# A two-layer token mixer on one core: other byte distances between matrix operands, other places for some halves, and row statistics by other instructions

## Chip, core and metric

The kernel runs on one core of a Trainium2 chip. The metric is the device time of one execution in microseconds (us); the kernel before takes 889.34 us, the median of 3 runs. The engines of the core are named as in the profile: PE is TensorE's matrix multiply and PEld its weight load, DVE is VectorE, ACT is ScalarE, POOL is GpSimd and SP the engine that issues most loads.

## What is computed

The reference runs two layers on 512 tokens of width 1024 (`x`) and, in the first layer, on 256 context tokens (`ctx`). Layer 0 is a retention mixer with four heads, layer 1 a gated mixer. Cut to what matters:

```
h  = rmsnorm(x, g) * (1 + scale) + shift            # per layer, from the conditioning vector
# layer 0, per head: q, k (256 wide), v, z (512 wide) = h @ w_in
o  = (q k^T * decay) v ;  o = o / rms(o) ;  x += gate * ((o * silu(z)) @ w_out)
# layer 1: u, v, z (2048 wide each) = h @ w_in
v  = v - mean(v, axis=-1)                            # over all 2048 columns of a token
v  = v * rsqrt(mean(v * v, axis=-1) + 1e-6) * vnorm_g
mixed = w_s[group] @ v[chunk of 128 tokens] + b_s
x += gate * ((u * mixed * silu(z)) @ w_out)
out = rmsnorm(x, final_g)
```

All inputs, weights and the output are float32.

## The kernel before

**Products.** A large product is made of seven half-size products of sums and differences of quarters (B11, B21, T1, T2, B22, T3, T4; a name that begins with T takes a difference of two weight quarters). Every float32 operand is split into a high part, rounded to the format that PE reads (a copy by ACT), and a low part, the rest (a subtraction by DVE); `mm3` then issues three matmuls: low by high, high by low, high by high. A weight quarter is loaded into a raw tile (`w0` and so on), for a T name subtracted on DVE, and split into one of four `hl` tiles. `Stream.get` (`Q.get`) hands the tiles out in order and keeps two more in preparation.

**Two forms.** `Product` (`features`, for q/k and for u/z of layer 1) keeps the weights stationary and streams 256 columns of activations. `Pair` (`tokens`, for v and z of layer 0 and v of layer 1, called V01, Z01, V23, Z23 and V1 below) keeps the activations (`oA..`, `oS..`, `hc`, and `rows` for the context) stationary and streams 512 columns of the split weight. The probabilities by v (`ph`, `pl` by `v`) and the last projection (`ya`, `yb` by `hl`) also stream 512 columns. `Pair.ended` copies banks by ACT into `snap` tiles (KEPT), adds to them by DVE (MADE) and calls `done`; for the quarter "21" the bank itself is handed over.

**Where tiles lie.** The loop over `(tag, size, bufs)` at the head of the kernel reserves SBUF in that order, sizes in float32 elements per partition. Counted from the first `hl` tile, modulo 256 bytes: an `hl` room has 8448 bytes, 33 times 256, so all four start at 0, and the split weight starts `FORMS` elements behind that: 32 bytes for kq, u and wo, 96 for v, z and v1, 128 for o. The eleven `t2` tiles (`snap`, `ph`, `pl`, `vt`, ...) are at 0; `cv` takes 64 bytes; so all `o..` tiles, `hc`, `g2`, `g3`, `s0`, `s2`, `s3` and `w4` are at 64, and behind `gate0` (32 bytes) `s1`, `rope`, the other `w` tiles and `dec` are at 96.

**Order.** PE follows the order of the text (`pe.kept = True`). From the end of the first stage on ACT and DVE do not (`act.kept = dve.kept = False`): a scheduler orders their instructions by the text as far as their operands and tiles are free, except behind `fence`. A tile that takes over the place of another one waits until the other one's last reader in the text is done.

**Places the change touches.** In V01 the sums of quarters come between the products (`sums`): `sum_s4` and `rows_s2` at T1, `sum_s3` at T2. The context rows lie in `w7` (S1), `s1` (S2), `s3` (S4) and `s0` (S3). The quarters of the activations lie in `s0` to `s3`: f11 in `s0`, f12 in `s1`, f21 in `s2`, f22 in `s3`; `sum_s3` subtracts f21 from f11 and is the last reader of f21. `load_qk(0)` and `load_v(0)` are generators that load and split (`halves`) q, k and v of head 0: they are stepped by `aside` during Z23 and, for what is left, at the first steps of `attend(0)`. `load_qk` has three steps of loads and five of halves, `load_v` four of loads and three of halves. In V1 `v1_done` puts two `bn_stats` of DVE per bank into a list (`measured`), which the loop over `TURNS1` works off; behind the loop come `bn_aggr`, a square root on ACT, a reciprocal and `nb`; `norm_vt(0)` scales the first v tiles, which the first pass over u multiplies behind its product B22.

Of the kernel before, what the change touches and what calls it, by code (L numbers as in the profile page):

```python
# [68 lines left out]
def hybrid_kernel(ctx, tc, xT_d, cT_d, cv_d, sv_d, rows_d, ada0_d, adag_d, w_d, rope_d, dec_d, ws_d, id_d, out_d):  # L69
# [13 lines left out]
    def st(shape, tag, dt=F32, bufs=1, name=None):  # L83
        return sb.tile(shape, dt, tag=tag, name=name or tag, bufs=bufs)

    T2 = 11
    HL = 4
    FORMS = {"kq": 8, "u": 8, "wo": 8, "v": 24, "z": 24, "v1": 24, "o": 32}


    for tag, size, bufs in (("hl", 2112, HL), ("t2", 512, T2), ("cv", 16, 1),
                            *((f"o{k}", 2048, 1) for k in ("A11", "A12", "A22", "S1", "S2", "S3", "S4")), ("hc", 4096, 1),
                            *((k, 1024, 1) for k in ("g2", "g3", "s0", "s2", "s3", "w4")), ("gate0", 8, 1),
                            *((k, 1024, 1) for k in ("s1", "rope", "w5", "w6", "w0", "w1", "w2", "w3", "w7", "g1", "g0")), ("dec", TW, 1)):
        st([P, size], tag, bufs=bufs, name="room")
# [43 lines left out]
    class Stream:  # L139
# [3 lines left out]
        def __init__(self):  # L143
            self.items, self.loads, self.raws, self.left, self.tiles = [], [], {}, {}, {}
            self.free, self.stage, self.done, self.sent, self.at = [], 0, 0, 0, -1
            self.gate = self.limit = self.cap = None
# [65 lines left out]
            return self.tiles.pop(self.at)  # L212

    Q = Stream()
    W = [f"w{i}" for i in range(7)]
    Q.free += W + ["g0"]

    def narrow_parts(a, b, kh):
# [160 lines left out]
    class Pair:  # L379

        def __init__(self, done, rows=None):
            self.done, self.rows, self.s, self.banks = done, rows, {}, {}

        def run(self, name, c, w):
            role = ROLE.get(name, "x")
# [15 lines left out]
        def ended(self, name, t, bank):  # L403
            if name in KEPT:
                k = self.s[KEPT[name], t] = t2("snap")
                act.copy(k, bank)
            elif name in MADE:
                key, to = MADE[name]
                k = self.s.pop((key, t))
                dve.tensor_tensor(k, bank, k, ALU.add)  # L410
                self.done(to, t, k)
            else:
                self.done("21", t, bank)
# [15 lines left out]
            load(xq[t, g], xT_d[:, 4 * g:4 * g + 4, t * HS:t * HS + HS])  # L429

    ada_w = {}
    ADA_AT = ("oS1", "oS2", "oS4", "oA22", "oS1", "oS2", "oS4", ("w7", "g1"))

    def ada0_load(kb):
        at = ADA_AT[kb]
# [357 lines left out]
    def rows_s1():  # L793
        dve.tensor_tensor(c22, c21, c22, ALU.add)
        dve.tensor_tensor(shc, sh0[:, 0:4, 1], sh0[:, 4:8, 1], ALU.add)
        rows_shifted("S1", "w7", shc)

    def rows_s2():
        dve.tensor_tensor(c22, c22, c11, ALU.subtract)
        rows_shifted("S2", "s1", sh0[:, 4:8, 1])  # L800

    def rows_s4():
        dve.tensor_tensor(c12, c12, c22, ALU.subtract)
# [194 lines left out]
    for q, name in TURNS:  # L998
        if q not in prods:
            prods[q] = project(q)  # L1000
            if q == Z23:
                Q.free.append("g0")
                qk0, v0 = load_qk(0), load_v(0)
        for c, unit in enumerate(units(q)):
            i = turn[q] = turn.get(q, -1) + 1
            if q[0] == "kq":
                prods[q].run(name, Q.get())
            else:
                prods[q].run(name, c, Q.get())
            if q == V01:  # L1010
                for made in sums.get((name, c), ()):
                    made()
                if c and name not in ("B11", "T1"):
                    popped()
                continue
            if i % 2:
                popped()
            if 1 not in pieces and (i % 2 if q == Z01 else q == V23 or i == 0):
                pieces.append(step())
            if q == V23 and i in (6, 8, 10, 12):  # L1020
                if i == 6:
                    dec0 = decay(0, ("g0", "s2"))
                aside(dec0)
            if q == Z23:
                if i in (0, 1, 2, 5, 7, 9):
                    aside(qk0)
                if i in (2, 4, 6, 11, 12):
                    aside(v0)
        if (q, name) == (V01, "T4"):
            Q.free.remove("g0")  # L1030
# [6 lines left out]
    def attend(h, qs, vs):  # L1037
# [83 lines left out]
        for i in range(len(steps) + LAG):  # L1121
            if i < len(steps):
                score(*steps[i])
            if i >= LAG:
                pv(*steps[i - LAG])
            if i == 2:
                aside(table())
            aside(qs)
            if i > 4 or h == 0 and i < 2:
                aside(vs)  # L1130
            if i == len(steps):
                flip()
            if (h, i) == (0, 2):
                for c in range(4):
                    load(acc[:, 2 * c:2 * c + 2, :], xT_d[:, 2 * c:2 * c + 2, :])
            if i < 5:
                aside(wo)
            if i in (3, 5, 6) or (h and i == 7):
                step()
# [149 lines left out]
    project_out(wos.pop(HEADS - 1), og, flip, (), then=half_sum, between=first_half, prepare=prepare)  # L1289


    bns = st([P, NT, 8, 6], "bns")
    measured = []

    def v1_done(p):
        def done(name, t, c):
            if name == "21":
                k = t2("snap")
                act.copy(k, c)
                c = k  # L1300
            n, nh = 2 * (int(name[0]) - 1) + t, int(name[1]) - 1
            measured.append(lambda: [dve.bn_stats(bns[:, n, 4 * p + 2 * j + nh, :], c[:, j * HS:j * HS + HS]) for j in range(2)])
            spill(vt_d[p][nh][:, :, n, :], c.rearrange("p (j n) -> p j n", j=2))
        return done

    rest1 = second_half()
    pairs = [Pair(v1_done(p)) for p in range(2)]
    for p, name in TURNS1:
        for c in range(2):
            pairs[p].run(name, c, Q.get())  # L1310
            while len(measured) > (4 if (p, name) in [(0, n) for n in PAIRED[:-1]] else 0):
                measured.pop(0)()
            if p == 0 and (c == 0 and name in ("B11", "B21", "T1", "T2", "B22") or (name, c) == ("B11", 1)):
                next(rest1)
        if (p, name) == (0, "B21"):
            residual()
# [3 lines left out]
    load(wsT, ws_d)  # L1320
    fg = st([P, D], "g0", name="fg")
    load(fg, rows_d[1:2, :].partition_broadcast(P))

    mv = st([P, NT, 2], "mv")
    for t in range(NT):
        dve.bn_aggr(mv[:, t, :], bns[:, t, :, :])
    rv = st([P, NT], "rv")
    act.activation(rv, mv[:, :, 1], AF.Sqrt, bias=eps, scale=1.0)
    dve.reciprocal(rv, rv)

    o1 = [st([P, D], f"s{t}", name="o1") for t in range(NT)]
    ya = st([P, 4, 2, SEQ], "hc", F32R, name="ya")
# [92 lines left out]
    def load_vt(i):  # L1425
        vts[i] = []
        for th in range(2):
            v = t2("vt", (P, 2, HS))
            load(v, vt_d[i // 4][i % 2][:, i // 2 % 2, 2 * th:2 * th + 2, :])
            vts[i].append(v)  # L1430

    nb = st([P, NT], "nb")
    dve.scalar_tensor_tensor(nb, mv[:, :, 0], -1.0, rv, ALU.mult, ALU.mult)

    def norm_vt(i):
        for n in range(NT):
# [26 lines left out]
        split((y[:, 0, :], y[:, 1, :]), a)  # L1463

    load_vt(0)
    norm_vt(0)
    for i in range(UZ):
        got, pms = {}, {}
        prod = Product(features, got.__setitem__)
        for name in SINGLE:  # L1470
            w = Q.get()
            settle()
            prod.run(name, w)
            if i < UZ - 1:
                if name == "T1":
                    load_vt(i + 1)
                if name == "T4":
                    norm_vt(i + 1)
# [122 lines left out]
```

## Time and profile before

| | |
|---|---|
| median of 3 runs | 889.34 us (889.31 to 889.42) |
| the profiled execution | 890.13 us, of it 888.4 us from the first to the last instruction |
| granted PE clock | 0.999 |
| PE / PEld / DVE / ACT busy | 98% / 88% / 81% / 52% of the span |
| DMA | 153.78 MB, 173 GB/s on average |

The profiled execution is 0.8 us longer than the median, 0.1%. All instructions carry line 55, the helper that records them, so groups are told apart by their tiles (written tile, then read ones) and shapes. The duration of a matmul is its own passage through the array; the next one starts before it ends, so the cost of one in a row of them is the distance between two starts: a block of n matmuls that is shown with its length lasts n - 1 such spacings and one duration.

### The profile page before, as it was taken

To read this page: it belongs to the slowest core of one execution; us is meant where nothing else is said; L and a number is where in the kernel's file an instruction comes from. 1 tells how busy PE (TensorE), PEld (TensorE's weight loads), DVE (VectorE), ACT (ScalarE), POOL (GpSimd) and SP (SyncE) were. 2 spreads that over 40 slices of the span, in tenths; PEclk is the share of its full clock that TensorE was granted. 3 is DMA by queue.
4 is the path that set the end of the run, shared out by engine and by line. 5 is a ranking of instruction groups with operands and counts; after the bars stand their busy time and mean duration, and the time that the engine had idled before them with its cause. 6 is when DMAs were issued, how large, how long until landed. Compare 5 with 4: busy or idle time off the path is not lost.

```text
span 888.4 us, 14615 instructions
## 1 busy us (share of the span) xinstructions
PE 873.1 (98%) x5670; PEld 778.8 (88%) x5670; DVE 722.8 (81%) x1016; ACT 463.1 (52%) x727; POOL 55.8 (6%) x92
## 2 busy tenths in 40 slices
PE   8999999999999999999999999999999999999997
PEld 7888898898889888999989898878999899899895
DVE  2689979988796977878687869999898578778986
ACT  5465444544524566536462559563765455255244
POOL 0001110110121020000000011102000000000000
PEclk9999999999999999999999999999999999999999
DMA  9931761972794586758175721546345045045202
GB/s 334 390 124 52 251 218 56 300 248 87 241 350 145 196 290 198 263 162 299 47 253 177 243 73 72 164 144 213 127 135 168 24 144 167 23 143 198 88 25 94
DMA packets 77092, 153.78 MB, mean 173 GB/s; under 512 B 8032, under 2 KB 35040, under 8 KB 77024
## 3 DMA queue, kind: packets, MB, share of 16 engines
q1 hardware_dynamic: 69888, 130.63, 44.9%
q0 software_dynamic: 6848, 22.03, 6.6%
q8 instruction: 44, 0.72, 0.4%
q10 hardware_dynamic: 288, 0.20, 0.1%
q14 instruction: 24, 0.20, 0.1%
HBM read 128.71 MB, written 24.12 MB: 172 GB/s over the span
## 4 chain that ended last, share of the span: by engine, by line
PE 88%; DVE 6%; ACT 3%; DMA 2%; issue 1%; SPq 0%; ACTq 0%; DVEq 0%
PE pst L55 88%; DVE hl L55 2%; DMA xq<-in_xT_dram 2%; DVE o L55 1%; DVE raw L55 1%; ACT hl L55 1%; DMA xs<-x 1%; DVE bns L55 1%; ACT f L55 0%; ACT oA L55 0%; ACT junk L55 0%; DVE ya L55 0%; DVE xq L55 0%; SPq L129 0%; ACT o L55 0%
## 5 line engine op out<-in xcount | busy, mean ns | idle before, releaser
L55 DVE TENSOR_TENSOR hl<-raw,hl 128x1024 fp32r<-128x1024 f32 x195 | 236.2, 1221 | 67.3 <-ACT hl L55 66.5
L55 ACT CAST hl<-raw 128x1024 fp32r<-128x1024 f32 x195 | 203.7, 1050 | 160.2 <-PE pst L55 63.5
L55 PE MATMUL pst<-hl,oS 128*128 128x512 f32 x576 | 137.9, 395 | 0.0
L55 PE MATMUL pst<-oS,hl 128*128 128x256 f32 x1104 | 134.7, 280 | 2.4 <-DVE hl L55 1.8
L55 PEld LDWEIGHTS pst<-oS,hl 128*128 128x128 f32 x1104 | 131.2, 188 | 3.6 <-DVE hl L55 2.2
L55 PEld LDWEIGHTS pst<-hl,oS 128*128 128x128 f32 x576 | 107.7, 187 | 27.0 <-DVE oS L55 0.4
L55 PE MATMUL pst<-oA,hl 128*128 128x256 f32 x936 | 118.2, 281 | 0.2
L55 PEld LDWEIGHTS pst<-oA,hl 128*128 128x128 f32 x936 | 112.8, 188 | 2.4 <-issue 0.8
L55 DVE TENSOR_TENSOR raw<-raw 128x1024 f32<-128x1024 f32 x92 | 111.3, 1219 | 0.8
L55 PE MATMUL pst<-hl,oA 128*128 128x512 f32 x408 | 98.6, 395 | 1.4 <-DVE hl L55 1.4
L55 PEld LDWEIGHTS pst<-hl,oA 128*128 128x128 f32 x408 | 76.0, 187 | 19.9 <-DVE hl L55 1.9
L55 PE MATMUL pst<-og,hl 128*128 128x256 f32 x768 | 92.8, 280 | 0.0
L55 PEld LDWEIGHTS pst<-og,hl 128*128 128x128 f32 x768 | 90.9, 188 | 0.8 <-issue 0.4
L55 ACT COPY snap<-pst 128x512 f32<-128x512 f32 x88 | 51.5, 587 | 70.1 <-PE pst L55 69.9
L55 PE MATMUL pst<-hl,ya 128*128 128x512 f32 (+1 forms) x300 | 69.4, 384 | 0.0
L55 PEld LDWEIGHTS pst<-hl,ya 128*128 128x128 f32 x300 | 54.7, 188 | 11.5
L55 PE MATMUL pst<-v,ph 128*128 128x512 f32 x192 | 59.7, 392 | 0.0
L55 DVE TENSOR_TENSOR snap<-pst,snap 128x512 f32<-128x512 f32 x75 | 51.2, 687 | 9.6 <-PE pst L55 9.0
L55 PEld LDWEIGHTS pst<-v,ph 128*128 128x128 f32 x192 | 36.1, 188 | 7.5
L55 ACT CAST ph<-pf 128x512 fp32r<-128x512 f32 x24 | 14.9, 622 | 51.0 <-DVE pf L55 48.3
L55 PE MATMUL pst<-v,pl 128*128 128x512 f32 x96 | 38.2, 398 | 0.0
L55 PEld LDWEIGHTS pst<-qk 128*128 128x128 f32 x288 | 35.8, 188 | 2.7 <-issue 1.6
(186 smaller groups left out, 990.6 us busy)
## 6 DMA issues: line engine op xcount, KB each, us to landing
raw<-in_w_dram SPq DMA_DIRECT2D x224, 256.0 KB, 4.3
bg<-in_adag_dram SPq DMA_DIRECT2D x32, 512.0 KB, 5.1
ada_w<-in_ada_dram SPq DMA_DIRECT2D x16, 512.0 KB, 8.9
raw<-in_w_dram SPq DMA_DIRECT2D x16, 512.0 KB, 3.9
bg<-in_dec_dram SPq DMA_DIRECT2D x12, 512.0 KB, 5.1
v<-snap POOLq DMA_DIRECT2D x16, 256.0 KB, 4.7
z<-snap POOLq DMA_DIRECT2D x16, 256.0 KB, 5.4
v<-v SPq DMA_DIRECT2D x8, 512.0 KB, 5.0
```

The source lines that it names most:

```text
L55: made = op(*args, **kw)
```

## The change

Five parts. (1) `FORMS` puts the split weights of v, z, v1 and o at element 16 (64 bytes), and `cv` is reserved ahead of `t2`, so `t2` tiles lie at 64 as well; the rows S1 and S2 move to `w4` and `s2`, both at 64. Every stationary tile that is used with 512 streamed columns then lies at the same place modulo 256 bytes as the streamed one ("row distance 0"). (2) `w7` and `w4` change roles in the list of raw tiles and in the first stage's loads, and the decay table of head 0 passes through `g0` and `s1`. (3) The remaining halves of q and k of head 0 (two steps) and one more of v are called at step 12 of Z23, and `attend(0)` steps `vs` at its first step only, not at two. (4) In V1 the sum of a block's 512 columns comes out of the addition that makes it (`scalar_tensor_tensor` with `accum_out`), or out of ACT's copy for "21"; ACT squares each block around the block's own mean with an accumulator (`AF.Square`, 16 of them) in place of 32 `bn_stats`. (5) Mean and variance are put together by `spread_v`, called behind T2 of the first pass over u together with `norm_vt(0)`; what is left in `measured` is worked off one per turn, and at that T2 all of it.

```diff
@@ -85,10 +85,10 @@
 
     T2 = 11
     HL = 4
-    FORMS = {"kq": 8, "u": 8, "wo": 8, "v": 24, "z": 24, "v1": 24, "o": 32}
-
-
-    for tag, size, bufs in (("hl", 2112, HL), ("t2", 512, T2), ("cv", 16, 1),
+    FORMS = {"kq": 8, "u": 8, "wo": 8, "v": 16, "z": 16, "v1": 16, "o": 16}
+
+
+    for tag, size, bufs in (("hl", 2112, HL), ("cv", 16, 1), ("t2", 512, T2),
                             *((f"o{k}", 2048, 1) for k in ("A11", "A12", "A22", "S1", "S2", "S3", "S4")), ("hc", 4096, 1),
                             *((k, 1024, 1) for k in ("g2", "g3", "s0", "s2", "s3", "w4")), ("gate0", 8, 1),
                             *((k, 1024, 1) for k in ("s1", "rope", "w5", "w6", "w0", "w1", "w2", "w3", "w7", "g1", "g0")), ("dec", TW, 1)):
@@ -212,7 +212,7 @@
             return self.tiles.pop(self.at)
 
     Q = Stream()
-    W = [f"w{i}" for i in range(7)]
+    W = ["w0", "w1", "w2", "w3", "w7", "w5", "w6"]
     Q.free += W + ["g0"]
 
     def narrow_parts(a, b, kh):
@@ -380,8 +380,8 @@
 
 
 
-        def __init__(self, done, rows=None):
-            self.done, self.rows, self.s, self.banks = done, rows, {}, {}
+        def __init__(self, done, rows=None, total=None):
+            self.done, self.rows, self.total, self.s, self.banks = done, rows, total, {}, {}
 
         def run(self, name, c, w):
             role = ROLE.get(name, "x")
@@ -407,7 +407,10 @@
             elif name in MADE:
                 key, to = MADE[name]
                 k = self.s.pop((key, t))
-                dve.tensor_tensor(k, bank, k, ALU.add)
+                if self.total:
+                    dve.scalar_tensor_tensor(k, bank, 0.0, k, ALU.add, ALU.add, accum_out=self.total(to, t))
+                else:
+                    dve.tensor_tensor(k, bank, k, ALU.add)
                 self.done(to, t, k)
             else:
                 self.done("21", t, bank)
@@ -429,7 +432,7 @@
             load(xq[t, g], xT_d[:, 4 * g:4 * g + 4, t * HS:t * HS + HS])
 
     ada_w = {}
-    ADA_AT = ("oS1", "oS2", "oS4", "oA22", "oS1", "oS2", "oS4", ("w7", "g1"))
+    ADA_AT = ("oS1", "oS2", "oS4", "oA22", "oS1", "oS2", "oS4", ("w4", "g1"))
 
     def ada0_load(kb):
         at = ADA_AT[kb]
@@ -793,11 +796,11 @@
     def rows_s1():
         dve.tensor_tensor(c22, c21, c22, ALU.add)
         dve.tensor_tensor(shc, sh0[:, 0:4, 1], sh0[:, 4:8, 1], ALU.add)
-        rows_shifted("S1", "w7", shc)
+        rows_shifted("S1", "w4", shc)
 
     def rows_s2():
         dve.tensor_tensor(c22, c22, c11, ALU.subtract)
-        rows_shifted("S2", "s1", sh0[:, 4:8, 1])
+        rows_shifted("S2", "s2", sh0[:, 4:8, 1])
 
     def rows_s4():
         dve.tensor_tensor(c12, c12, c22, ALU.subtract)
@@ -1019,12 +1022,12 @@
                 pieces.append(step())
             if q == V23 and i in (6, 8, 10, 12):
                 if i == 6:
-                    dec0 = decay(0, ("g0", "s2"))
+                    dec0 = decay(0, ("g0", "s1"))
                 aside(dec0)
             if q == Z23:
-                if i in (0, 1, 2, 5, 7, 9):
+                for _ in range({0: 1, 1: 1, 2: 1, 5: 1, 7: 1, 9: 1, 12: 2}.get(i, 0)):
                     aside(qk0)
-                if i in (2, 4, 6, 11, 12):
+                for _ in range({2: 1, 4: 1, 6: 1, 11: 1, 12: 2}.get(i, 0)):
                     aside(v0)
         if (q, name) == (V01, "T4"):
             Q.free.remove("g0")
@@ -1126,7 +1129,7 @@
             if i == 2:
                 aside(table())
             aside(qs)
-            if i > 4 or h == 0 and i < 2:
+            if i > 4 or h == 0 and i < 1:
                 aside(vs)
             if i == len(steps):
                 flip()
@@ -1289,26 +1292,37 @@
     project_out(wos.pop(HEADS - 1), og, flip, (), then=half_sum, between=first_half, prepare=prepare)
 
 
-    bns = st([P, NT, 8, 6], "bns")
+    vsum = st([P, NT, 4], "vsum")
+    vmid = st([P, NT, 4], "vmid")
+    vsq = st([P, NT, 4], "vsq")
     measured = []
+
+    def v1_total(p):
+        def total(name, t):
+            n, nh = 2 * (int(name[0]) - 1) + t, int(name[1]) - 1
+            return vsum[:, n, 2 * p + nh:2 * p + nh + 1]
+        return total
 
     def v1_done(p):
         def done(name, t, c):
+            n, b = 2 * (int(name[0]) - 1) + t, 2 * p + int(name[1]) - 1
             if name == "21":
                 k = t2("snap")
-                act.copy(k, c)
+                act.activation(k, c, AF.Copy, accum_out=vsum[:, n, b:b + 1])
                 c = k
-            n, nh = 2 * (int(name[0]) - 1) + t, int(name[1]) - 1
-            measured.append(lambda: [dve.bn_stats(bns[:, n, 4 * p + 2 * j + nh, :], c[:, j * HS:j * HS + HS]) for j in range(2)])
-            spill(vt_d[p][nh][:, :, n, :], c.rearrange("p (j n) -> p j n", j=2))
+            if t == 1:
+                dve.tensor_scalar(vmid[:, n - 1:n + 1, b], vsum[:, n - 1:n + 1, b], -1.0 / 512, None, ALU.mult)
+            measured.append(lambda: act.activation(t2("junk1"), c, AF.Square, bias=vmid[:, n, b:b + 1], scale=1.0,
+                                                   accum_out=vsq[:, n, b:b + 1]))
+            spill(vt_d[p][int(name[1]) - 1][:, :, n, :], c.rearrange("p (j n) -> p j n", j=2))
         return done
 
     rest1 = second_half()
-    pairs = [Pair(v1_done(p)) for p in range(2)]
+    pairs = [Pair(v1_done(p), total=v1_total(p)) for p in range(2)]
     for p, name in TURNS1:
         for c in range(2):
             pairs[p].run(name, c, Q.get())
-            while len(measured) > (4 if (p, name) in [(0, n) for n in PAIRED[:-1]] else 0):
+            if len(measured) > (4 if p == 0 else 2):
                 measured.pop(0)()
             if p == 0 and (c == 0 and name in ("B11", "B21", "T1", "T2", "B22") or (name, c) == ("B11", 1)):
                 next(rest1)
@@ -1320,13 +1334,6 @@
     load(wsT, ws_d)
     fg = st([P, D], "g0", name="fg")
     load(fg, rows_d[1:2, :].partition_broadcast(P))
-
-    mv = st([P, NT, 2], "mv")
-    for t in range(NT):
-        dve.bn_aggr(mv[:, t, :], bns[:, t, :, :])
-    rv = st([P, NT], "rv")
-    act.activation(rv, mv[:, :, 1], AF.Sqrt, bias=eps, scale=1.0)
-    dve.reciprocal(rv, rv)
 
     o1 = [st([P, D], f"s{t}", name="o1") for t in range(NT)]
     ya = st([P, 4, 2, SEQ], "hc", F32R, name="ya")
@@ -1429,8 +1436,21 @@
             load(v, vt_d[i // 4][i % 2][:, i // 2 % 2, 2 * th:2 * th + 2, :])
             vts[i].append(v)
 
+    rv = st([P, NT], "rv")
     nb = st([P, NT], "nb")
-    dve.scalar_tensor_tensor(nb, mv[:, :, 0], -1.0, rv, ALU.mult, ALU.mult)
+
+    def spread_v():
+        mean = st([P, NT], "mean")
+        var = st([P, NT], "var")
+        dve.tensor_reduce(mean, vsum, axis=AX.X, op=ALU.add)
+        dve.tensor_scalar(mean, mean, 1.0 / 2048, None, ALU.mult)
+        dve.tensor_tensor(vmid, vmid, mean.unsqueeze(2).to_broadcast([P, NT, 4]), ALU.add)
+        dve.tensor_tensor(vmid, vmid, vmid, ALU.mult)
+        dve.scalar_tensor_tensor(vsq, vmid, 512.0, vsq, ALU.mult, ALU.add)
+        dve.tensor_reduce(var, vsq, axis=AX.X, op=ALU.add)
+        act.activation(rv, var, AF.Sqrt, bias=eps, scale=1.0 / 2048)
+        dve.reciprocal(rv, rv)
+        dve.scalar_tensor_tensor(nb, mean, -1.0, rv, ALU.mult, ALU.mult)
 
     def norm_vt(i):
         for n in range(NT):
@@ -1463,7 +1483,6 @@
         split((y[:, 0, :], y[:, 1, :]), a)
 
     load_vt(0)
-    norm_vt(0)
     for i in range(UZ):
         got, pms = {}, {}
         prod = Product(features, got.__setitem__)
@@ -1471,6 +1490,13 @@
             w = Q.get()
             settle()
             prod.run(name, w)
+            if measured:
+                measured.pop(0)()
+            if i == 0 and name == "T2":
+                while measured:
+                    measured.pop(0)()
+                spread_v()
+                norm_vt(0)
             if i < UZ - 1:
                 if name == "T1":
                     load_vt(i + 1)
```

## Prediction

> **What bounds the kernel now.** I read the page first, then the waits of PE.
>
> ```profile
> PE 873.1 (98%) x5670; PEld 778.8 (88%) x5670; DVE 722.8 (81%) x1016; ACT 463.1 (52%) x727; POOL 55.8 (6%) x92
> ```
>
> ```profile
> PE pst L55 <- DVE hl L55: 3.2, 3, 1.4
> PE pst L55 <- issue: 1.4, 1, 1.4
> ```
>
> PE is busy for 98% of the span, and its waits add up to a few us, of which three of about 1.4 us are most. So time can come from two sources: the spacing of PE's matmuls, and these three waits. For the spacing I took the groups with shapes kept apart (each the number of its matmuls behind the x) and then blocks of the timeline.
>
> ```profile
> L55 PE MATMUL pst<-hl,oS 128*128 128x512 f32 x576 | 137.9, 395 | 0.0
> ...
> L55 PE MATMUL pst<-hl,oA 128*128 128x512 f32 x408 | 98.6, 395 | 1.4 <-DVE hl L55 1.4
> ...
> L55 PE MATMUL pst<-hl,ya 128*128 128x512 f32 x276 | 66.6, 394 | 0.0
> L55 PE MATMUL pst<-v,ph 128*128 128x512 f32 x192 | 59.7, 392 | 0.0
> L55 PE MATMUL pst<-v,pl 128*128 128x512 f32 x96 | 38.2, 398 | 0.0
> ```
>
> ```profile
> L55 PE MATMUL pst<-hl,rows 128*128 128x512 f32 x96 | 24.7, 392 | 0.0
> L55 PE MATMUL pst<-hl,yb 128*128 128x512 f32 x96 | 24.6, 391 | 0.0
> ```
>
> ```profile
> L55 PE MATMUL pst<-hl,hc 128*128 128x512 f32 x72 | 18.7, 395 | 0.0
> ```
>
> In the kernel before, `rows` S1 and S2 (in `w7`, `s1`, at 96) meet an `hl` at 96, distance 0, while `rows` S4 and S3 (`s3`, `s0`, at 64) meet it 32 bytes apart. The same holds within one pass, so it is an experiment that the old kernel makes by itself: below, the block at 92.02 is S2, that at 96.19 is S4.
>
> ```profile
> 92.02 1.53 PE L55 MATMUL pst<-hl,rows 128*128 128x512 f32 x6
> 93.39 2.96 PE L55 MATMUL pst<-hl,oS 128*128 128x512 f32 x12
> 96.19 1.56 PE L55 MATMUL pst<-hl,rows 128*128 128x512 f32 x6
> ```
>
> ```profile
> 537.44 2.90 PE L55 MATMUL pst<-hl_e,oA 128*128 128x512 f32 x12
> ```
>
> A block of n lasts n - 1 spacings and one duration of 0.39. S2: (1.53 - 0.393)/5 = 227.4 ns; S4: (1.56 - 0.393)/5 = 233.4 ns; the twelve at 93.39 (distance 32): (2.96 - 0.395)/11 = 233.2 ns. The `hl_e` tiles lie in `oA22` and `oS2`, at 64 like their `oA11`, so distance 0 again: (2.90 - 0.389)/11 = 228.3 ns. Last, the distance of 64 (`ya` with an `o` weight at 128, `v` at 64 with `ph`, `pl` at 0):
>
> ```profile
> 685.48 22.57 PE L55 MATMUL pst<-hl,ya 128*128 128x512 f32 x96
> ```
>
> ```profile
> 754.99 1.54 PE L55 MATMUL pst<-hl,ya 128*128 128x512 f32 x6
> ```
>
> ```profile
> 347.40 0.39 PE L55 MATMUL pst<-v,pl 128*128 128x512 f32 x1
> ```
>
> ```profile
> 350.17 1.57 PE L55 MATMUL pst<-qk 128*128 128x256 f32 x12
> ```
>
> (22.57 - 0.394)/95 = 233.4 ns, (1.54 - 0.394)/5 = 229.2 ns, and from 347.40 to 350.17 twelve in 2.77 us, 230.8 ns: between the two others, and not even.
>
> **The change part by part.**
>
> *Distances.* At 32 bytes today: 576 + 408 + 72 + half of the 96 `rows` = 1104 matmuls (the 24 `hl_e` are groups of their own). I take 227.7 for distance 0, between 227.4 and 228.3: 233.3 - 227.7 = 5.6 ns each, 6.2 us (bounds 5.0 and 6.0 ns: 5.5 to 6.6). At 64 bytes: 276 + 96 + 192 + 96 = 660, from about 230.5 to 227.7, 2.8 ns each, 1.8 us (bounds 0.9 and 6.0 ns: 0.6 to 4.0). Together 8.0 us. The 256-column forms (kq, u, wo) stay 32 apart and keep their spacing. `vt` and `gt` in `t2` change their distance to `wsT` and `ident`; these are 128 and 64 short matmuls that the rows above do not price, and at the 6 ns of the 512-column case either way they are 1.2 us at most; I take 0.
>
> The Trainium skill speaks against this part: "TensorE: Matmul & The Clock Gate", section "Step-by-step: what each phase is for", says that PE has two independent SBUF read ports, so that loading the next weights takes no bandwidth from the running matmul. By it the place of a tile would not matter. The trace disagrees: 1.53 against 1.56 us for six matmuls of equal shape in the same pass. What would come out if it held is the second rival.
>
> *What eats part of it.* DVE makes the `hl` tiles, and where it has no time left PE cannot go faster.
>
> ```profile
> 143.55:182.75 39.20, 39.20 (x171) 31.54 (x170) 38.04 (x44) 21.24 (x26) 5.76 (x10) 1.00 0.69 223
> 550.14:619.36 69.22, 67.80 (x290) 54.01 (x289) 65.25 (x91) 38.41 (x49) 9.92 (x15) 1.00 0.50 160
> ```
>
> Columns: stretch, length, busy PE, PEld, DVE, ACT, POOL. In Z01 (first row) DVE is busy 38.04 of 39.20 us and PE wants 168 x 5.6 ns = 0.9 us; I take off 0.4 (0 to 0.9). In V01 a new order arises: the rows S2 move into `s2`, where f21 lies until `sum_s3` has read it, so `rows_s2` must now wait for a subtraction that stood behind it.
>
> ```profile
> 85.10 1.14 DVE L55 SCALAR_TENSOR_TENSOR rows<-cq,sh,rows 128x128 fp32r<-128x128 f32 x4
> 86.15 1.22 DVE L55 TENSOR_TENSOR xq<-xq 128x1024 f32<-128x1024 f32 x1
> ```
>
> ```profile
> 84.39 1.28 ACT L55 ACTIVATE rows<-cq,sh 128x128 fp32r<-128x128 f32 x4
> ```
>
> ```profile
> 87.86 1.53 PE L55 MATMUL pst<-hl,rows 128*128 128x512 f32 x6
> ```
>
> Today the rows are done at 86.2 and wanted at 87.86. Then: the subtraction takes their place at 85.10 and ends at 86.3, ACT's four follow (1.28), DVE meanwhile makes one `hl` (another 1.22, to 87.5) and then the first two rows, enough for the first half of the product, at about 88.1. PE, faster by some 108 x 5.6 ns = 0.6 us by then, wants them at 87.2 and waits 0.9 us: the 0.6 and 0.3 more are lost. Bounds: 0 if the scheduler pulls the subtraction further ahead, 2.6 us if it stays at 86.15 (87.4 + 1.28 + 1.14 = 89.8, less 87.2). I take 0.9. Behind PE, which waits, nothing else is late: its other operands are made already. For the last projections, where DVE adds and gates every bank, 0.2. Left of the 8.0: 6.5 us.
>
> *The wait at the start of attention.*
>
> ```profile
> 333.21 2.96 PE L55 MATMUL pst<-qk 128*128 128x256 f32 x24
> 337.58 1.64 PE L55 MATMUL pst<-qk 128*128 128x256 f32 x12 [1.41 <-issue]
> ```
>
> ```profile
> 334.81 0.69 DVE L55 SCALAR_TENSOR_TENSOR pf<-pst,dt 128x512 f32<-128x512 f32 x1 [3.45 <-PE pst L55]
> 336.19 0.69 DVE L55 TENSOR_TENSOR pl<-pf,ph 128x512 fp32r<-128x512 f32 x1 [0.69 <-ACT ph L55]
> 336.80 0.69 DVE L55 TENSOR_TENSOR qk<-qk 128x512 fp32r<-128x512 f32 x1
> ```
>
> The third score block takes the context's keys; their low half is made at 336.80, behind `pf` and `pl`, and PE goes on when it ends. With the halves called at step 12 of Z23 this lies where DVE sat idle for 3.45 us. What is late next is the bank: `pf` of the first block ends at 335.50, before PE is through with the second; then `pl`, at 336.88, before PE is through with the third. So the 1.41 goes; the added ACT and DVE work (three halves, moved and not new) lies in idle time.
>
> *The two waits of V1.*
>
> ```profile
> 575.80 2.70 DVE L55 BATCH_NORM_STATS2 bns<-snap 128x6 f32<-128x256 f32 x8
> ```
>
> ```profile
> 583.09 2.83 PE L55 MATMUL pst<-hl,oA 128*128 128x512 f32 x11 [1.41 <-DVE hl L55]
> ```
>
> ```profile
> 622.37 0.59 DVE L55 BATCH_NORM_AGGREGATE mv<-bns 128x2 f32<-128x48 f32 x2
> ```
>
> ```profile
> 626.49 3.09 PE L55 MATMUL pst<-oS,hl 128*128 128x256 f32 x24 [1.36 <-DVE hl L55]
> ```
>
> Eight statistics in a row stand ahead of the splits that PE waits for at 583.09; statistics and aggregation stand ahead of those that it waits for at 626.49. The prices:
>
> ```profile
> L55 DVE BATCH_NORM_STATS2 bns<-snap 128x6 f32<-128x256 f32 x32 | 11.4, 414 | 0.1
> ```
>
> ```profile
> L55 ACT ACTIVATE junk<-o 128x512 f32<-128x512 f32 x7 | 4.4, 633 | 6.4 <-DVE o L55 6.4
> L55 ACT ACTIVATION_READ_ACCUMULATOR junk<-o 128x1 f32 x9 | 1.7, 187 | 0.0
> ```
>
> DVE loses 32 statistics, 11.4 us. It gains 8 tiny `vmid`, 8 operations of `spread_v` at about 0.17 (as `nb` and the reciprocal are now), some 3 us with a reading of the accumulator at each of the 12 additions (no such reading on DVE is in the trace; bounds 0 and ACT's 0.19 each, I take the half); in V1 it is then busy some 57 of 69 us. ACT gains 16 x (0.633 + 0.187) = 13.1 us, on 38.41 of 69.22. Both fit. The deadline of the new chain is the first use of `vt`:
>
> ```profile
> 637.92 1.95 PE L55 MATMUL pst<-wsT,vt 128*128 128x128 f32 x16
> ```
>
> `spread_v` is called behind T2, which ends near 629 today; about 1.5 us of small DVE steps and a root, and four scalings of 0.6, are done some 4 us ahead of 637.92. I take both waits as gone, 1.41 + 1.36; with the 1.41 above that is 4.2 us, less 0.2 for what shows up in their place: 4.0.
>
> **Sum.** 6.5 + 4.0 = 10.5 us from the profiled execution's 890.13 gives 879.6; the median stands 0.8 lower, so **878.8 us**.
>
> **The rivals.**
>
> 1. *New waits take the place of the old ones in V1 and u* (the squares stand ahead of a cast that PE needs, `vt` comes late), so that only the distances and the start of attention pay: 6.5 + 1.4 = 7.9, 881.4; without the latter too, 882.8. For it: at the passage from V1 to u DVE is just in time today. Against: DVE gets 8 us lighter there. 0.14.
>
> 2. *The distance is not the cause*, and S2 against S4 differ by something else. Then only the waits go: 4.2 us, 885.1. For it: the distance of 64 is uneven (229.2 to 233.4). Against: two places at distance 0, in two stages and with different tiles, both at 228 or below 228.4. 0.09.
>
> 3. *Slower.* ACT follows its queue; if every one of the 16 squares stood ahead of a cast whose tile PE is about to take, each would cost its 0.82 us: 13.1 us, more than the whole gain, 891.9. It decides from the 13th on (10.5/0.82). Against: ACT is idle for 31 of 69 us there, and tiles are made two ahead. 0.04.
>
> 4. *More*: 6.0 ns on all 1764 matmuls (10.6 us), nothing eaten, the full 4.2 us: 14.8, 874.5. 0.05.
>
> **How the numbers follow.** The forecast, 876 to 881.4 with the bounds of its terms, has 0.68; rival 1 0.14, 2 0.09, 3 0.04, 4 0.05. The range from 875.3 to 884.0 holds the forecast and rival 1 and leaves out 2, 3 and most of 4. A measurement of this kernel tells 0.2%, 1.8 us, from no change. Faster by more than that: 0.96; within it 0.01; slower 0.03, since rival 3 in part gives no change.
>
> **What would show it.** Right: blocks of six `rows` or twelve `hl,oS` with 1.53 and 2.90 in place of 1.56 and 2.96; the last score block of three without its 1.41; PE's waits for `hl` near 0; a new wait of PE for `rows` of up to 1 us near 87. Wrong: blocks that stay at 2.96 (rival 2), or [..<-DVE hl] and waits for `vt` between 575 and 640 (rival 1), or ACT's squares ahead of late casts (rival 3).

## The result, and the profile after

The changed kernel takes 876.84 us (median of 4 runs, 876.66 to 877.05) beside 889.33 us for the one before: a ratio of 0.986, interval 0.9843 to 0.9877. That is 12.5 us off, where 10.5 were forecast. Its profiled execution took 876.77 us, of it 875.0 us from the first to the last instruction, so this time the profile lies at the median, while the one before lay 0.8 above it: the spans differ by 13.4 us, the medians by 12.5.

The busy time of each engine, from the page after:

```profile
PE 862.8 (99%) x5670; PEld 777.7 (89%) x5670; DVE 712.8 (81%) x1006; ACT 472.3 (54%) x763; POOL 55.9 (6%) x92
```

The same 5670 matmuls now keep PE busy for 862.8 us in place of 873.1. The rest of the gain is time in which PE stood still. Two rows of its waits after (what it waited for: us in total, times, the longest); each of the others comes to about 1 us or less in both kernels, and most of that lies in the first 60 us:

```profile
PE pst L55 <- DVE rows L55: 0.7, 1, 0.7
PE pst L55 <- DVE hl L55: 0.6, 1, 0.6
```

The wait by "issue" of 1.4 us is gone, of three waits for `hl` with 3.2 us one with 0.6 us is left, and one wait for `rows` is new. First the spacing, in the groups after with shapes kept apart:

```profile
L55 PE MATMUL pst<-hl,oS 128*128 128x512 f32 x576 | 134.3, 390 | 0.1
...
L55 PE MATMUL pst<-hl,oA 128*128 128x512 f32 x408 | 95.8, 390 | 0.0
...
L55 PE MATMUL pst<-hl,ya 128*128 128x512 f32 x276 | 65.6, 389 | 0.0
...
L55 PE MATMUL pst<-v,pl 128*128 128x512 f32 x96 | 37.9, 395 | 0.0
```

The 576 of `oS` lost 3.6 us, 6.3 ns each, the 408 of `oA` 2.8 us, 6.9 ns each, the 276 of `ya` 1.0 us, 3.6 ns each, and p by v (`pl`) 0.3 us. The same in V01, where the new order of the rows S2 is seen as well; PE's timeline after (start, length, operation and count, idle time ahead and what ended it):

```profile
82.73 1.52 PE L55 MATMUL pst<-hl,rows 128*128 128x512 f32 x6
84.09 2.88 PE L55 MATMUL pst<-hl,oS 128*128 128x512 f32 x12
87.69 1.66 PE L55 MATMUL pst<-hl,rows 128*128 128x512 f32 x6 [0.72 <-DVE rows L55]
89.18 2.89 PE L55 MATMUL pst<-hl,oS 128*128 128x512 f32 x12
91.91 1.52 PE L55 MATMUL pst<-hl,rows 128*128 128x512 f32 x6
```

Twelve of `oS` last 2.88 us: (2.88 - 0.390)/11 = 226.4 ns, where it was 233.2. The join behind the first of them takes 3.60 us from start to start, the one behind the second 2.73; with the `rows` block itself 0.13 longer than its neighbour (1.49 against 1.36 to the next start) the new wait costs 1.0 us. DVE's and ACT's timelines after show why:

```profile
84.41 1.22 DVE L55 TENSOR_TENSOR xq<-xq 128x1024 f32<-128x1024 f32 x1
...
86.15 1.22 DVE L55 TENSOR_TENSOR hl<-raw,hl 128x1024 fp32r<-128x1024 f32 x1
87.28 1.14 DVE L55 SCALAR_TENSOR_TENSOR rows<-cq,sh,rows 128x128 fp32r<-128x128 f32 x4
```

```profile
84.77 2.00 ACT L55 CAST hl<-raw 128x1024 fp32r<-128x1024 f32 x2
86.67 1.27 ACT L55 ACTIVATE rows<-cq,sh 128x128 fp32r<-128x128 f32 x4
```

The subtraction (`xq`) frees `s2` at 85.6; ACT is busy with two casts until 86.7 and then writes the rows, DVE makes one `hl` meanwhile and then the rows' low part; PE goes on when the first of these four is there.

PE's timeline after at the two other places, the start of attention and V1 with its passage to u:

```profile
328.79 4.36 PE L55 MATMUL pst<-qk 128*128 128x256 f32 x36
```

```profile
565.57 11.04 PE L55 MATMUL pst<-hl,oA 128*128 128x512 f32 x48
576.45 21.92 PE L55 MATMUL pst<-hl,oS 128*128 128x512 f32 x96
...
609.10 2.96 PE L55 MATMUL pst<-oA,hl 128*128 128x256 f32 x24
611.90 5.76 PE L55 MATMUL pst<-oS,hl 128*128 128x256 f32 x48
```

The three score blocks run as one of 36, V1's blocks of 48 and the 48 of u without a break. By stage, from the starts of the same matmuls in both traces:

| stage | change, us |
|---|---|
| up to V01 | -0.35 |
| V01 | -0.24 |
| Z01, V23, Z23 | -1.08, -1.40, -1.11 |
| attention of head 0, the three others | -1.79, -0.14 each |
| V1 | -3.61 |
| first passes over u | -1.95 |
| the four parts of the last projection | -0.60, -0.20, -0.21, -0.18 |
| the wait ahead of the last pass over u | +0.20 |

Each stage of layer 0 that streams 512 columns pays, V01 hardly, since its 1.2 us go back to the rows. The table leaves out stages with smaller changes, 0.5 us together. Its first row lies ahead of every step that was argued; the waits for loads there differ from one kernel to the next, and it wasn't tried apart.

### The profile page after: what moved, and what is told of

The parts are those of the page before. It is cut to its first block, busy times and chain, and to the rows that moved or that the text cites. A ratio compares the mean times of both kernels' runs of the same rounds, so it can differ in the third digit from the quotient of the medians.

```text
span 875.0 us, 14637 instructions
## 1 busy us (share of the span) xinstructions
PE 862.8 (99%) x5670; PEld 777.7 (89%) x5670; DVE 712.8 (81%) x1006; ACT 472.3 (54%) x763; POOL 55.9 (6%) x92
## 4 chain that ended last, share of the span: by engine, by line
PE 86%; DVE 8%; ACT 3%; DMA 2%; issue 1%; SPq 0%; DVEq 0%; ACTq 0%
PE pst L55 86%; DVE hl L55 2%; DVE o L55 2%; DMA xq<-in_xT_dram 2%; DVE raw L55 1%; ACT hl L55 1%; DVE xq L55 1%; DVE ya L55 1%; ACT f L55 1%; DVE oS L55 0%; ACT oA L55 0%; ACT junk L55 0%; DVE cq L55 0%; DVE snap L55 0%; ACT oS L55 0%
## 5 line engine op out<-in xcount | busy, mean ns | idle before, releaser
L55 PE MATMUL pst<-hl,oS 128*128 128x512 f32 x576 | 134.3, 390 | 0.1
L55 PE MATMUL pst<-hl,oA 128*128 128x512 f32 x408 | 95.8, 390 | 0.0
L55 ACT COPY snap<-pst 128x512 f32<-128x512 f32 x84 | 48.9, 585 | 50.0 <-PE pst L55 48.9
L55 DVE TENSOR_TENSOR snap<-pst,snap 128x512 f32<-128x512 f32 x63 | 42.5, 687 | 5.1 <-PE pst L55 5.0
L55 DVE SCALAR_TENSOR_TENSOR acc<-pst,gate,acc 128x256 f32<-128x256 f32 x64 | 29.1, 479 | 10.9 <-PE pst L55 10.7
L55 PE MATMUL pst<-v,pl 128*128 128x512 f32 x96 | 37.9, 395 | 0.0
```

Of the source, the lines that this page charges most:

```text
L55: made = op(*args, **kw)
```

## The experiments

Each kernel below was run on a chip together with the kernel before, whose median was between 889.94 and 890.21 us on the three chips used, so kernels of different chips are compared by their ratios.

### Each part alone

**Parts 1 and 2 alone** (the places in memory; halves and statistics as before):

```diff
-    FORMS = {"kq": 8, "u": 8, "wo": 8, "v": 24, "z": 24, "v1": 24, "o": 32}
+    FORMS = {"kq": 8, "u": 8, "wo": 8, "v": 16, "z": 16, "v1": 16, "o": 16}
...
-        rows_shifted("S2", "s1", sh0[:, 4:8, 1])
+        rows_shifted("S2", "s2", sh0[:, 4:8, 1])
```

> Parts 1 and 2 alone (FORMS, cv ahead of t2, rows S1 and S2, raw tiles); halves and statistics as before. Theory (the distance of the two operands modulo 256 bytes sets the spacing): all blocks with 512 columns at 227 ns, 8.4 us in all, less 1.0 us for the wait for the rows S2 and up to 1 us that grows onto the two waits of V1, which stay: 881.5 to 883. Rival (the distance is not the cause, the gain is that of the waits): 889 to 890, with the wait for the rows S2 even slower.

Measured: 882.57 us (882.46 to 882.70) beside 890.0, ratio 0.9919 (0.9902 to 0.9935): 7.4 us. Z01, V23 and Z23 gain 1.08, 1.42 and 1.11 us as in the whole change. PE's waits in this kernel:

```profile
PE pst L55 <- DVE hl L55: 3.6, 3, 1.7
PE pst L55 <- issue: 1.4, 1, 1.4
...
PE pst L55 <- DVE rows L55: 0.7, 1, 0.7
```

All three old waits are there, those for `hl` grew from 3.2 to 3.6 us: a faster PE reaches the late tile sooner. So a stall takes back part of what the spacing gains, until the stall itself goes; V1 gains 1.62 us here against 3.61 in the whole.

**Part 3 alone** (the halves at step 12 of Z23):

```diff
-                if i in (0, 1, 2, 5, 7, 9):
+                for _ in range({0: 1, 1: 1, 2: 1, 5: 1, 7: 1, 9: 1, 12: 2}.get(i, 0)):
...
-            if i > 4 or h == 0 and i < 2:
+            if i > 4 or h == 0 and i < 1:
```

> Part 3 alone: the halves of q, k and v of head 0 called in Z23. Theory (the third score block waits for the low half of the context's keys): the one wait at 337 goes, 1.6 us counted from start to start, nothing else moves: 887.7. Rival (another wait takes its place, for the score banks or for pl): 889.

Measured: 888.13 us (887.67 to 889.02) beside 890.0, ratio 0.998 (0.997 to 0.9989): 1.9 us. PE's timeline in this kernel:

```profile
333.06 4.37 PE L55 MATMUL pst<-qk 128*128 128x256 f32 x36
```

The 36 run through; the head's attention is 1.67 us shorter, and no new wait shows up in its place.

**Parts 4 and 5 alone** (statistics by sums and by ACT, with their new pacing and place):

```diff
-            measured.append(lambda: [dve.bn_stats(bns[:, n, 4 * p + 2 * j + nh, :], c[:, j * HS:j * HS + HS]) for j in range(2)])
+            measured.append(lambda: act.activation(t2("junk1"), c, AF.Square, bias=vmid[:, n, b:b + 1], scale=1.0,
+                                                   accum_out=vsq[:, n, b:b + 1]))
...
-            while len(measured) > (4 if (p, name) in [(0, n) for n in PAIRED[:-1]] else 0):
+            if len(measured) > (4 if p == 0 else 2):
```

> Parts 4 and 5 alone: sums and squares in place of the statistics, mean and variance behind T2 of the first pass over u; distances and halves as before. Theory (32 statistics on DVE stood ahead of the splits): both waits, at 583 and 626, go, 1.6 and 1.6 us from start to start, and some tenths of the short waits behind them: 885.8. Rival (the waits go only because the distances moved the work): at most 1 us, 888 or more.

Measured: 886.5 us (886.12 to 887.14) beside 890.0, ratio 0.9963 (0.9949 to 0.9976): 3.5 us; V1 gains 1.70 and the first passes over u 1.59. The three parts alone give 7.4 + 1.9 + 3.5 = 12.8 us, the whole 12.5: they add up. Each theory of where the time comes from held so far; the two questions left are whether the distance is what counts in the first part, and what counts in the last.

### Is it the distance?

**Everything moved by 32 bytes**, all distances as in the changed kernel: a room of 32 bytes ahead of `hl`.

```diff
-    for tag, size, bufs in (("hl", 2112, HL), ("cv", 16, 1), ("t2", 512, T2),
+    for tag, size, bufs in (("pad", 8, 1), ("hl", 2112, HL), ("cv", 16, 1), ("t2", 512, T2),
```

> The changed kernel with 32 bytes reserved ahead of everything, so that every tile moves by 32 bytes and every distance stays. Theory (the distance counts): 876.8, blocks with 512 columns at 227 ns. Rival (the place itself counts, 64 bytes behind a multiple of 256): the 512-column blocks go back to 233 ns, 885.

Measured: 876.62 us (876.47 to 876.99) beside 890.0, ratio 0.9852 (0.9838 to 0.9867). The group of `oS` in this kernel:

```profile
L55 PE MATMUL pst<-hl,oS 128*128 128x512 f32 x576 | 134.2, 390 | 0.1
```

Same busy time to 0.1 us: the place itself, as far as a shift of 32 bytes tells, doesn't count, the distance does.

**The 512-column forms 128 bytes apart** (the probabilities by v stay at distance 0):

```diff
-    FORMS = {"kq": 8, "u": 8, "wo": 8, "v": 16, "z": 16, "v1": 16, "o": 16}
+    FORMS = {"kq": 8, "u": 8, "wo": 8, "v": 48, "z": 48, "v1": 48, "o": 48}
```

> The changed kernel with v, z, v1 and o at element 48: the 1476 token and output blocks with 512 columns lie 128 bytes from their stationary tiles, the products with v keep distance 0. Theory A (only distance 0 is free, all else pays as 32 bytes does): 233 ns, 1476 x 6 = 9 us slower, 885.5. Theory B (the penalty is for neighbours within 64 bytes, farther is free): 227 ns, 876.8. In between, as 64 bytes did (229 to 233 ns): 880 to 883.

Measured: 885.17 us (884.8 to 885.52) beside 890.21, ratio 0.9942 (0.9926 to 0.9959): the gain of the first part is gone. Two groups of this kernel:

```profile
L55 PE MATMUL pst<-hl,oS 128*128 128x512 f32 x576 | 137.5, 395 | 0.0
...
L55 PE MATMUL pst<-v,pl 128*128 128x512 f32 x96 | 37.9, 395 | 0.0
```

`oS` is back to within 0.4 us of the kernel before (137.9), p by v, whose distance stayed 0, keeps its 37.9. Of 0, 32 and 128 bytes only 0 is fast for 512 columns. No kernel had the stationary tile above the streamed one at 512 columns, so the side was not tried there.

At 64 bytes, where the last projection and p by v lie in the kernel before, the distance alone does not settle the spacing. The 96 `ya` at 685.48 last 22.57 us in that kernel and in those of part 3 alone and of parts 4 and 5 alone; in the kernel with the spreading alone (below), which moves no tile, they last 22.15:

```profile
682.63 22.15 PE L55 MATMUL pst<-hl,ya 128*128 128x512 f32 x96
```

That is (22.15 - 0.394)/95 = 229.0 ns in place of 233.4. The last block of `ya` changes the other way: 22.23 us in the kernel before, 22.59 in the three others. What decides between the two is open. So blocks at 64 bytes can shift a time by some 0.4 us each with nothing changed in them.

**The 256-column forms at distance 0 too**, where the change leaves the stationary tile 32 bytes below the streamed one:

```diff
-    FORMS = {"kq": 8, "u": 8, "wo": 8, "v": 16, "z": 16, "v1": 16, "o": 16}
+    FORMS = {"kq": 16, "u": 16, "wo": 16, "v": 16, "z": 16, "v1": 16, "o": 16}
```

> The changed kernel with kq, u and wo at element 16 too, so that the forms that stream 256 columns also have distance 0 (2800 of the 2954 such pairs). Theory as it stands says nothing of 256 columns; the 23 such pairs at distance 0 in the changed profile have 119.7 ns against 116.7 at 32 bytes. If these stand for all: 2800 x 3.0 = 8.4 us slower, 885.2. Rival (distance 0 is best for every shape, as for 512 columns): 2800 x 3 ns faster, 868.

Measured: 885.7 us (885.57 to 885.75) beside 890.21, ratio 0.9947 (0.9933 to 0.9962), beside 0.986 for the changed kernel; its profiled span is 883.9 us, 8.9 longer. The groups of `oS` with 256 columns, first in the changed kernel, then in this one:

```profile
L55 PE MATMUL pst<-oS,hl 128*128 128x256 f32 x1104 | 134.3, 280 | 1.2 <-DVE hl L55 0.6 <-ACT oS L55 0.5
```

```profile
L55 PE MATMUL pst<-oS,hl 128*128 128x256 f32 x1104 | 137.8, 284 | 0.9 <-ACT oS L55 0.4 <-DVE hl L55 0.4
```

3.5 us more for 1104 matmuls, 3.2 ns each. What is best for 512 columns is bad for 256. Is 32 below the best for these? Three more kernels set "kq", "u" and "wo" to 24 (32 bytes above the streamed tile), 0 (64 below) and 48 (128 apart):

```diff
-    FORMS = {"kq": 8, "u": 8, "wo": 8, "v": 16, "z": 16, "v1": 16, "o": 16}
+    FORMS = {"kq": 24, "u": 24, "wo": 24, "v": 16, "z": 16, "v1": 16, "o": 16}
```

> The changed kernel with kq, u and wo at element 24: the stationary weight lies 32 bytes behind the streamed tile (96 against 64) where it now lies 32 bytes ahead of it (32 against 64). If only the amount of the distance counts for 256 columns: 116.7 ns, 876.7. If its sign counts: anything from 113 ns (the lowest that is common now; 2800 x 3.7 = 10 us faster, 866.5) to 120 ns (885.7, as at distance 0).

> The changed kernel with kq, u and wo at element 0: the stationary weight lies 64 bytes ahead of the streamed tile. If the 256-column spacing is best at 32 bytes and grows to both sides: 118 ns (the 23 pairs at 64 bytes in the old profile had 117.9), 880. If any distance other than 0 is as good: 876.7.

> The changed kernel with kq, u and wo at element 48: the two operands lie 128 bytes apart. The 23 pairs of 256 columns that lay 128 apart in the run before last had 120.2 ns: if these stand for all, 2800 x 3.5 = 9.8 us slower, 886.5. If any distance other than 0 is as good: 876.7.

Measured, beside 889.94: 881.09 us, ratio 0.9902 (0.9887 to 0.9917), with 32 above; 879.83 us, ratio 0.9887 (0.9871 to 0.9904), with 64 below; 883.7 us, ratio 0.993 (0.9916 to 0.9945), with 128. The group of `oS` with 256 columns in the three, in this order:

```profile
L55 PE MATMUL pst<-oS,hl 128*128 128x256 f32 x1104 | 136.0, 281 | 1.1 <-ACT oS L55 0.5 <-DVE hl L55 0.5
```

```profile
L55 PE MATMUL pst<-oS,hl 128*128 128x256 f32 x1104 | 135.1, 280 | 1.3 <-DVE hl L55 0.6 <-ACT oS L55 0.5
```

```profile
L55 PE MATMUL pst<-oS,hl 128*128 128x256 f32 x1104 | 137.1, 283 | 0.9 <-ACT oS L55 0.4 <-DVE hl L55 0.3
```

Busy time by 1104: 121.6 ns with 32 below, 122.4 with 64 below, 123.2 with 32 above, 124.2 with 128, 124.8 with 0. It is no matter of equal or unequal alone: the side counts, and 128 lies between what either theory said of it. The kernel as changed has the best of the five.

### Is it the engine, or the order?

The prediction gave the two waits of V1 to DVE's load: 32 statistics on an engine that was full. But parts 4 and 5 change three things: which engine works, how the work is spread over the turns, and where the end is computed. **The statistics back on DVE, everything else as changed**, so with the new spreading and the aggregation behind T2:

```diff
-            measured.append(lambda: act.activation(t2("junk1"), c, AF.Square, bias=vmid[:, n, b:b + 1], scale=1.0,
-                                                   accum_out=vsq[:, n, b:b + 1]))
+            measured.append(lambda: [dve.bn_stats(bns[:, n, 2 * b + j, :], c[:, j * HS:j * HS + HS]) for j in range(2)])
...
-    pairs = [Pair(v1_done(p), total=v1_total(p)) for p in range(2)]
+    pairs = [Pair(v1_done(p)) for p in range(2)]
```

> The changed kernel with the 32 statistics back on DVE, but in the new pacing (one pair per turn, the rest behind V1, mean and variance behind T2 of u) and without the sums and squares. Theory (DVE's load is what PE waited for): waits for hl come back in V1 and at the passage to u, 1 to 3 us: 878 to 880. Rival (only the clumps of eight statistics and their place ahead of the splits made the waits; the engine is not short of time): 877, no change.

Measured: 876.55 us (876.28 to 876.83) beside 890.21, ratio 0.9845 (0.983 to 0.986). The theory fell. The page of this kernel, and its DVE timeline where the kernel before had eight statistics in a row:

```profile
PE 863.3 (99%) x5670; PEld 778.3 (89%) x5670; DVE 722.1 (83%) x1016; ACT 460.9 (53%) x727; POOL 55.9 (6%) x92
```

```profile
575.31 1.21 DVE L55 TENSOR_TENSOR hl<-raw,hl 128x1024 fp32r<-128x1024 f32 x1
576.43 0.42 DVE L55 BATCH_NORM_STATS2 bns<-snap 128x6 f32<-128x256 f32 x1
576.77 1.21 DVE L55 TENSOR_TENSOR raw<-raw 128x1024 f32<-128x1024 f32 x1
577.89 0.75 DVE L55 BATCH_NORM_STATS2 bns<-snap 128x6 f32<-128x256 f32 x2
```

DVE is 9.3 us busier than in the changed kernel, ACT 11.4 us less busy, and the span is the same 875.0 us. The statistics stand singly and in twos between the splits, and PE has no wait there.

**The kernel before with the spreading alone**: statistics on DVE, the aggregation at its old place, nothing else changed.

```diff
-            while len(measured) > (4 if (p, name) in [(0, n) for n in PAIRED[:-1]] else 0):
+            if len(measured) > (4 if p == 0 else 2):
                 measured.pop(0)()
...
+    while measured:
+        measured.pop(0)()
```

> The kernel before with one edit: the statistics of V1 are worked off one pair per turn, as the squares are in the changed kernel, and what is left at its end ahead of the aggregation, which stays where it was. If the clump of eight statistics made the wait at 583: that wait goes and the one at 626 stays, 1.6 us, 888.0 beside 889.6. If DVE's load made it: it stays or comes back some turns later, 889.6.

Measured: 886.77 us (886.36 to 887.36) beside 889.94, ratio 0.9966 (0.9953 to 0.9979): 3.2 us, about what parts 4 and 5 gave (0.9963). By stage V1 gains about 1.7 us and the first passes over u 1.4, where parts 4 and 5 gave 1.70 and 1.59. Two of PE's waits, two stretches of DVE's timeline and a block of PE's in this kernel:

```profile
PE pst L55 <- issue: 1.4, 1, 1.4
...
PE pst L55 <- DVE hl L55: 0.4, 1, 0.4
```

```profile
575.36 0.74 DVE L55 BATCH_NORM_STATS2 bns<-snap 128x6 f32<-128x256 f32 x2
576.02 1.21 DVE L55 TENSOR_TENSOR raw<-raw 128x1024 f32<-128x1024 f32 x1
577.15 0.74 DVE L55 BATCH_NORM_STATS2 bns<-snap 128x6 f32<-128x256 f32 x2
...
617.18 1.16 DVE L55 TENSOR_TENSOR hl<-raw,hl 128x1024 fp32r<-128x1024 f32 x1
618.26 1.39 DVE L55 BATCH_NORM_STATS2 bns<-snap 128x6 f32<-128x256 f32 x4
619.57 0.58 DVE L55 BATCH_NORM_AGGREGATE mv<-bns 128x2 f32<-128x48 f32 x2
```

```profile
620.68 6.12 PE L55 MATMUL pst<-oS,hl 128*128 128x256 f32 x48
```

One changed condition, with a loop for what is left at the end, takes the first wait away and most of the second. (The 0.4 us for `hl` lie ahead of the last pass over u, as in the kernel before.) DVE is as full as it was, busy for 65.47 of the 67.28 us from 550.60 to 617.88, nearly all of V1, and PE does not wait there: the clump made the first wait. Of the second, 0.3 us is left: the 48 of u last 6.12 us, 5.81 with parts 4 and 5 alone. That it goes so far was not expected, since the aggregation hadn't moved. The split that PE needs at that point stands behind the last statistics and the aggregation in both kernels, about 3.5 us from the end of the aggregation to PE's next start. But the aggregation ends 3.6 us after the first matmul of u in the kernel before (622.96 against 619.36) and 2.3 us after it here (620.15 against 617.88), since after the 24th statistic three splits and one subtraction of weights stand ahead of its end, where there were four and two. Why the scheduler orders them so wasn't tried apart.

### Can the new wait for the rows be had back?

**The subtraction f11 - f21 one turn earlier**, behind B21 in place of T2, otherwise as changed:

```diff
+    def take_s3():
+        dve.tensor_tensor(f11, f11, f21, ALU.subtract)
+
     def sum_s3():
         op("S3")
-        dve.tensor_tensor(f11, f11, f21, ALU.subtract)
...
```

> The changed kernel with the subtraction f11 - f21 of sum_s3 taken one turn earlier, behind B21, so that s2 is free when the rows S2 are made. Theory (PE waits for the rows S2, which wait for that subtraction): the wait of 0.7 us and its restart go, 0.97 us: 875.9. Rival (DVE is full there, and the subtraction only pushes another split late): 876.8.

Measured: 877.5 us (877.23 to 878.1) beside 890.21, ratio 0.9856 (0.9842 to 0.9871), no better than the 876.55 of the kernel with paced statistics on the same chip, which has the wait. A row of PE's waits and one of its timeline in this kernel:

```profile
PE pst L55 <- DVE hl L55: 1.6, 2, 1.0
```

```profile
89.84 2.79 PE L55 MATMUL pst<-hl,oS 128*128 128x512 f32 x11 [1.05 <-DVE hl L55]
```

The wait for `rows` went, and one of 1.05 us for `hl` stands right behind its place (the second row is PE's timeline); V01 is 0.33 us longer than in the changed kernel. DVE has no room in that stretch (it is busy for all of the 34 us from 76 to 110, here and in the changed kernel), so that an operation pulled ahead pushes a split back.

No kernel tried is measurably faster than the changed one: the moved one and the one with paced statistics on DVE come within what a measurement tells.

## Why the prediction was right, and where it wasn't

**Distances: the mechanism right, the size low.** 227.7 ns was taken for distance 0; twelve `oS` of V01 after show 226.4, and the means over the groups of `oS`, `oA` and `hc` lie between 226.7 and 227.5. So 6.3 ns in place of 5.6 at 1104 matmuls, 7.0 us in place of 6.2. The 660 at 64 bytes gave 0.5 us in attention and 1.2 us in the last projection, 1.7 for the 1.8 forecast; that these agree is partly luck, since the last projection of the kernel before has blocks of both spacings, 229.0 and 233.4, and which block has which differs from kernel to kernel. The sum, 8.7, lies a little above the 8.0 and within the bounds of that step. The experiments show that the distance does it: moved as a whole the tiles keep the gain, set 128 bytes apart they lose it. The Trainium skill, "TensorE: Matmul & The Clock Gate", section "Step-by-step: what each phase is for", has weights and moving data read through independent ports; for the time of these matmuls the traces disagree, by 6.3 ns of 233.

**What eats part of it: two right, one wrong.** The rows' wait came where it was described, and with the subtraction pulled ahead (the last experiment) it goes; 0.9 forecast, 1.0 measured. That the size fits is partly luck: DVE began the subtraction at 84.41, 0.7 us ahead of the 85.10 that was taken, but ACT, whose turn was counted from the end of the subtraction, had two casts to finish first and began the rows 1.0 us after that end. The 0.2 of the last projections is there as well, in the wait ahead of the last pass over u. The 0.4 taken off in Z01, since DVE was busy for 38.04 of 39.20 us, wasn't lost: Z01 gained 1.08 us, all of 168 x 6.3 = 1.06. The busy share of DVE alone didn't limit PE there.

**The start of attention: right.** The wait went; the bank and `pf` weren't late next.

**The two waits of V1: right that they go, wrong in the reason.** Here a step of the reasoning failed, though the time came out: "DVE loses 32 statistics" was given as what frees the splits. Statistics that stay on DVE, spread one pair at a time, free them nearly as well (0.9845 with everything else as changed, 0.9966 alone). What PE had waited for at 583.09 was the row that the prediction quoted itself, eight statistics in one piece ahead of the splits; the old condition asked for all that was left at the moment when p changes to 1. The Trainium skill, "Perfetto Trace Analysis", section "Optimizing Scalar/DVE Operations", holds that with a saturated DVE some work may be worth moving to Scalar; DVE was busy for 65.25 of 69.22 us, and here the move brought nothing that can be measured beside the order.

**The size of the waits.** Gaps of 1.41, 1.41 and 1.36 us were counted. From start to start they cost more: the join at 583.09 took 10.21 us for 37 matmuls that need 37 x 0.2333 = 8.63, so 1.58, and the first block behind a gap runs some 0.1 us longer. The three are worth 1.64, 1.68 and 1.61, together 4.9 where 4.2 less 0.2 was forecast. The 2 us between forecast and result are thus 0.9 from the waits, 0.7 from the distances and 0.4 from Z01.

**The new operations' prices.** The groups of V1 and the passage after:

```profile
L55 DVE SCALAR_TENSOR_TENSOR snap<-pst,snap 128x512 f32<-128x512 f32 x12 | 7.9, 688 | 0.3 <-PE pst L55 0.3
...
L55 DVE DVE_READ_ACCUMULATOR snap<-pst,snap 128x1 f32 x12 | 1.0, 86 | 0.0
...
L55 ACT ACTIVATE junk<-snap,vmid 128x512 f32<-128x512 f32 x16 | 11.5, 722 | 1.2 <-DVE vmid L55 1.2
...
L55 ACT ACTIVATION_READ_ACCUMULATOR junk<-snap,vmid 128x1 f32 x16 | 3.0, 190 | 0.0
```

The reading of DVE's accumulator takes 86 ns, near the half of ACT's that was taken. A square with its reading takes 0.91 us, not 0.82. Both lie beside other work.

**The rivals.** None decided: no new waits in V1 or u, the distance is the cause, and ACT, busy for 47.6 of the 67 us from 545 to 612, had room for the squares.

## What to carry to other kernels

Where PE is busy all the time, look at the spacing of its matmuls by operand pair: a kernel that has the same shape at two distances in memory has made the experiment already, and each streamed width needs its own, since the best distance for one was bad for another. Before work is moved off a full engine, look in the timeline for clumps of it ahead of what the bound engine waits for: spreading the clump may bring nearly the whole gain in one line. And count a gap from start to start, against the spacing of the rows beside it, not by its idle time alone.

## What was not expected of the hardware

Float32 matmuls of 512 columns whose weights are loaded meanwhile start about every 227 ns when streamed and stationary tile lie at the same place modulo 256 bytes, every 233 ns where the stationary one lies 32 bytes below, and the busy time at 128 bytes is nearly that high (137.5 us of `oS` in place of 137.9). At 64 bytes below, blocks of `ya` show 229.0 or 233.4 ns, and the same block can show either in two kernels that keep its tiles in place. At 256 columns it is nearly the other way round: 121.6 ns of busy time each with the stationary tile 32 bytes below, 124.8 ns at distance 0. No run shows what in the chip does this.
